# Down projections of the latents: one 512-column matmul for both parts of the input, halves added by VectorE

## The chip, the core and the metric

The kernel runs on one core of one Trainium2 chip. The metric is the device time of one execution in microseconds (us). A profiled execution gives the rows that are read below: TensorE matmuls (PE), TensorE weight loads (PEld), VectorE (DVE), ScalarE (ACT), GpSimd (POOL) and SyncE's DMA queue (SP). Each engine works through a queue of its own in a fixed order.

## What is computed

A two-layer backbone over 256 latent tokens and 256 context tokens of width 1024. Layer 0 mixes tokens by attention, layer 1 by a Fourier transform; each layer has a SwiGLU feed-forward before and one behind the mixing, so there are four feed-forwards. The first one treats latents and context, the other three the latents alone. The part that the change touches, cut from the reference:

```python
def swiglu(h, w_gu, w_d):
    g, u = jnp.split(h @ w_gu, 2, axis=-1)
    return (jax.nn.silu(g) * u) @ w_d

x = x + 0.5 * mx[2] * swiglu(modulate(rms_norm(x, norm_g[i, 0]), mx[0], mx[1]),
                             ffn1_w_gu[i], ffn1_w_d[i])
```

`w_gu` is 1024 x 5632 and `w_d` 2816 x 1024, in 32-bit floats. 2816 is 22 tiles of 128, called inner tiles here.

## The kernel before

**Products in parts.** TensorE works on rounded 32-bit operands. So that little is lost, each operand is split into a rounded part (`hi`, ScalarE's cast in `split`, L101) and the rest (`lo`, VectorE's subtraction, L102). A product is three matmuls into one bank of PSUM (`mm3`, L140 to L143): hi weights with the hi input, hi weights with the lo input, lo weights with the hi input. Each matmul loads its 128x128 block of weights anew, though the first two load the same block.

**A feed-forward** (`ffn`) runs in two halves of 11 inner tiles. In each half `gate_up` makes the 11 tiles of `silu(g) * u` (16 x 3 matmuls a tile, 258 columns: 256 tokens and two that carry the shift) and splits each into `h_hi` and `h_lo`. Then come eight down projections (`down`), one for each tile `dt` of the 1024 outputs: 11 x 3 matmuls of 256 columns into one bank (`dn`), and one VectorE instruction that multiplies the bank by the gate and adds it to the stream `xy` (L331). Such a run of eight down projections is called a down stretch here. The three feed-forwards of the latents alone have six of them.

**Behind the second half** of a feed-forward the next part waits for the stream: `after(dt)` scales the tile just finished into the next operand (`scaled`: `xop_hi` by ScalarE, L291, and `xop_lo` by VectorE, L292) and adds its square for the next norm (`sumsq`, ScalarE and GpSimd). Two places matter below. At the **first turn** the second feed-forward of layer 0 ends and the first of layer 1 begins: its `gate_up` needs all eight `xop` tiles. At the **second turn** that feed-forward ends and the Fourier mixing begins: it needs the norm's factors (`nv_l1m`, L251, made from the squares of all eight tiles).

**Beside it** VectorE splits the weights that come next (`wlo_d`, `wlo_gu`, `wlo_wf`: four instructions for each load), and works off the adaLN vectors of layer 1 (`products`, L193, named `junk` after its unused output: one instruction of 1024 columns for each 512 KB of the loaded `raw_m`). Raw weights, hi parts and lo parts live in rotating buffers: a DMA is issued when the buffer that it writes has been read.

**Order.** The program is written in the order above; the order in each engine's queue is set when the program is built, by a scheduler that follows estimated times and priorities (`URGENT` for the last additions to the stream, `AHEAD` for weights). On the chip each queue is strictly in order: an instruction that waits holds up all behind it.

Of the kernel before, what the change touches and what calls it, by code (L numbers as in the profile page):

```python
# [8 lines left out]
F32 = mybir.dt.float32  # L9
F32R = mybir.dt.float32r  # L10
# [4 lines left out]
P = 128  # L15
# [11 lines left out]
# first feed-forward: slices of its hidden tiles  # L27
SLICES = ((0, 6), (6, 12), (12, 17), (17, 22))
# order of the start: tiles of the first adaLN weights, xN pairs of input tiles, n norm, fN operands of a tile of d,
# gN first weights, c conditions  # L30
# [3 lines left out]
# adaLN work beside the feed-forwards: vectors of layer 1 done in the first one, VectorE time (us) per step, first tiles  # L34
# [6 lines left out]
# attention: slots of a head group's steps, offsets of the groups, order of the projections  # L41
# [5 lines left out]
# priorities of weight loads and of what the next phase waits for  # L47
AHEAD = 60
URGENT = 200
# pieces of a weight unit's split; buffers, lasting and added by phases  # L50
# [7 lines left out]
# columns of the packed small parameters (one row per partition)  # L58
# [5 lines left out]
# columns of the packed row vectors (broadcast to all partitions)  # L64
R_QG, R_KG, R_LQ1, R_LK1, R_LQ2, R_LK2 = range(0, 6 * HD, HD)
# columns of the shape-only tables
# [9 lines left out]
def tile_kernel(ctx: ExitStack, tc, xyT, small, rows, tables, w_mod0, w_mod, w_gu, w_d0, w_d, w_qkv, w_o, w_f, out):  # L76
# [22 lines left out]
    # ---------------------------------------------------------------- helpers  # L99
# [4 lines left out]
    # weights pass through rotating buffers; a phase that has the room adds some to the lasting ones  # L104
# [46 lines left out]
    # ---------------------------------------------------------------- constants, small inputs  # L151
# [13 lines left out]
    # ---------------------------------------------------------------- adaLN parameters  # L165
    mod = const.tile([P, 2, 2, 9, KT], F32, name="mod")  # layer, stream, which, d tile
    amul = const.tile([P, 2, 2, 3, KT], F32, name="amul")

    def first_products(dt, spool):
        """shift and scale of the first norm, both streams, for one tile of d: in rows"""  # L170
# [26 lines left out]
    def condition(sb, s):  # L197
        """silu of a condition, the same on all partitions"""
        nc.sync.dma_start(sb, rows[:, 6 * HD + s * D:6 * HD + (s + 1) * D].partition_broadcast(P))
        S.activation(sb, sb, AF.Silu)  # L200

    def ada_steps(pool, todo, conds):
        """one step per quarter of a vector's (transposed) weights"""
# [22 lines left out]
    # ---------------------------------------------------------------- norm pieces  # L226
    tails = {}  # the last d tile's squares
# [12 lines left out]
    def rstd_cols(acc, sl, name):  # L240
        """1/rms of each token, tokens on the partitions"""
# [668 lines left out]
```

## Time and profile before

| what | value |
|---|---|
| time, median of 3 runs | 1247.15 us (1245.64 to 1248.89) |
| span of the profiled execution | 1244.7 us |
| TensorE matmul busy | 1227.4 us (99%) |
| VectorE busy | 906.8 us (73%) |
| ScalarE busy | 549.3 us (44%) |

The times hold no separate time for the profiled execution; its span, from the first to the last instruction, is 2.4 us below the median. TensorE is busy nearly all the time as far as the page can say: ends of matmuls are modelled and overlap, so the distance between the starts of two matmuls tells more than the time of one. VectorE's 73% is a mean over stretches that differ.

### The profile page before, as it was taken

To read this page: it belongs to the slowest core of one execution; us is meant where nothing else is said; L and a number is where in the kernel's file an instruction comes from. 1 tells how busy PE (TensorE), PEld (TensorE's weight loads), DVE (VectorE), ACT (ScalarE), POOL (GpSimd) and SP (SyncE) were. 2 spreads that over 40 slices of the span, in tenths; PEclk is the share of its full clock that TensorE was granted. 3 is DMA by queue.
4 is the path that set the end of the run, shared out by engine and by line. 5 is a ranking of instruction groups with operands and counts; after the bars stand their busy time and mean duration, and the time that the engine had idled before them with its cause. 6 is when DMAs were issued, how large, how long until landed. Compare 5 with 4: busy or idle time off the path is not lost. (4 is left out here: it accounts for less than half of the span.)

```text
span 1244.7 us, 21253 instructions
## 1 busy us (share of the span) xinstructions
PE 1227.4 (99%) x8540; PEld 1121.5 (90%) x8540; DVE 906.8 (73%) x1761; ACT 549.3 (44%) x1207; POOL 102.0 (8%) x89
## 2 busy tenths in 40 slices
PE   9999999999999999999999999999999999999998
PEld 4688888888888889998899999999999999999998
DVE  1996985658874777777778687888688767766664
ACT  2342232223223455445645445555455545544552
POOL 1100000000001352340200000110000011000000
PEclk9999999999999999999999999999999999999999
DMA  9564574558881122122465686676686555536532
GB/s 364 217 239 166 204 248 136 198 184 308 314 309 68 69 102 102 69 68 69 170 223 198 234 302 226 211 301 227 211 310 240 171 195 183 180 127 244 189 117 81
DMA packets 37811, 241.94 MB, mean 194 GB/s; under 512 B 4224, under 2 KB 5376, under 8 KB 14672
## 3 DMA queue, kind: packets, MB, share of 16 engines
q1 hardware_dynamic: 37584, 240.25, 53.8%
q8 instruction: 67, 1.10, 0.3%
q0 software_dynamic: 128, 0.33, 0.2%
q14 instruction: 32, 0.26, 0.1%
HBM read 239.51 MB, written 1.05 MB: 193 GB/s over the span
## 5 line engine op out<-in xcount | busy, mean ns | idle before, releaser
L142 PE MATMUL gu<-xop_lo,whi_gu 128*128 128x258 f32 (+1 forms) x1408 | 440.2, 313 | 2.1 <-DVE xop_lo L292 2.1
L141 PE MATMUL gu<-xop_hi,whi_gu 128*128 128x258 f32 (+1 forms) x1408 | 439.0, 312 | 1.7 <-ACT whi_gu L101 1.4
L143 PE MATMUL gu<-xop_hi,wlo_gu 128*128 128x258 f32 (+1 forms) x1408 | 439.6, 312 | 0.4 <-DVE wlo_gu L102 0.2
L142 PEld LDWEIGHTS gu<-xop_lo,whi_gu 128*128 128x128 f32 x1408 | 268.0, 190 | 20.1 <-DVE xop_lo L292 2.6
L141 PEld LDWEIGHTS gu<-xop_hi,whi_gu 128*128 128x128 f32 x1408 | 268.0, 190 | 18.3 <-ACT whi_gu L101 1.7
L143 PEld LDWEIGHTS gu<-xop_hi,wlo_gu 128*128 128x128 f32 x1408 | 268.0, 190 | 17.2 <-DVE wlo_gu L102 1.3
L101 ACT CAST whi_gu<-raw_gu 128x512 fp32r<-128x512 f32 x352 | 194.7, 618 | 188.5 <-PE gu L142 102.4
L102 DVE TENSOR_TENSOR wlo_gu<-raw_gu,whi_gu 128x512 fp32r<-128x512 f32 x352 | 226.5, 689 | 60.1 <-ACT whi_gu L101 59.2
L142 PE MATMUL dn<-h_lo,whi_d 128*128 128x256 f32 (+1 forms) x724 | 219.6, 305 | 0.0
L143 PE MATMUL dn<-h_hi,wlo_d 128*128 128x256 f32 (+1 forms) x724 | 219.5, 305 | 0.0
L141 PE MATMUL dn<-h_hi,whi_d 128*128 128x256 f32 (+1 forms) x724 | 217.8, 305 | 0.2 <-DVE xy L331 0.2
L193 DVE SCALAR_TENSOR_TENSOR junk<-raw_m,cond_x 128x1024 f32<-128x1024 f32 x128 | 156.6, 1223 | 34.1 <-DMA raw_m<-in_w_mod 33.1
L101 ACT CAST whi_d<-raw_d 128x352 fp32r<-128x352 f32 (+2 forms) x256 | 105.9, 484 | 167.7 <-PE gu L142 84.5
L102 DVE TENSOR_TENSOR wlo_d<-raw_d,whi_d 128x352 fp32r<-128x352 f32 (+2 forms) x256 | 120.9, 524 | 58.6 <-ACT whi_d L101 58.6
L141 PEld LDWEIGHTS dn<-h_hi,whi_d 128*128 128x128 f32 x724 | 136.4, 189 | 6.8 <-PE dn L143 0.6
L142 PEld LDWEIGHTS dn<-h_lo,whi_d 128*128 128x128 f32 x724 | 136.9, 189 | 6.1
L143 PEld LDWEIGHTS dn<-h_hi,wlo_d 128*128 128x128 f32 x724 | 136.8, 189 | 6.1
L499 PE MATMUL pj<-whi_qkv,xop_hi 128*128 128x256 f32 x320 | 92.1, 288 | 0.6 <-DVE kr L545 0.5
L501 PE MATMUL pj<-whi_qkv,xop_lo 128*128 128x256 f32 x320 | 91.2, 286 | 1.4 <-DVE xop_lo L281 1.2
L331 DVE SCALAR_TENSOR_TENSOR xy<-dn,mod,xy 128x256 f32<-128x256 f32 x112 | 50.3, 477 | 57.5 <-PE dn L143 57.4
L500 PE MATMUL pj<-wlo_qkv,xop_hi 128*128 128x256 f32 x320 | 91.2, 285 | 0.9 <-DVE wlo_qkv L102 0.8
L101 ACT CAST h_hi<-hh 128x256 fp32r<-128x256 f32 (+1 forms) x88 | 40.3, 460 | 92.9 <-DVE hh L316 60.2
(220 smaller groups left out, 1412.5 us busy)
## 6 DMA issues: line engine op xcount, KB each, us to landing
raw_gu<-in_w_gu SPq DMA_DIRECT2D x88, 1024.0 KB, 5.2
raw_m<-in_w_mod SPq DMA_DIRECT2D x72, 1024.0 KB, 5.5
raw_d<-in_w_d SPq DMA_DIRECT2D x48, 704.0 KB, 4.1
raw_qkv<-in_w_qkv SPq DMA_DIRECT2D x12, 1024.0 KB, 4.8
raw_d<-in_w_d SPq DMA_DIRECT2D x8, 768.0 KB, 4.3
raw_d<-in_w_d SPq DMA_DIRECT2D x8, 640.0 KB, 5.3
raw_wo<-in_w_o SPq DMA_DIRECT2D x4, 1024.0 KB, 4.9
raw_wf<-in_w_f SPq DMA_DIRECT2D x4, 1024.0 KB, 6.9
```

The costliest lines, as they stand in the source:

```text
L101: S.copy(hi, src)
L102: V.tensor_sub(lo, src, hi.bitcast(F32))
L141: PE.matmul(ps, sh, mh, start=start, stop=False)
L142: PE.matmul(ps, sh, ml, start=False, stop=False)
L143: PE.matmul(ps, sl, mh, start=False, stop=stop)
L193: V.scalar_tensor_tensor(junk, w, 1.0, c, op0=ALU.mult, op1=ALU.mult, accum_out=out_col)
L331: V.scalar_tensor_tensor(xy[:, dt, so], ps[:, so.start - sl.start:so.stop - sl.start], mod[:, layer, s, 6 * f + 2, dt:dt + 1], xy[:, dt, s ...
L499: PE.matmul(ps[:, i], xh, wh, start=k == 0, stop=False)
L500: PE.matmul(ps[:, i], xh, wl, start=False, stop=False)
L501: PE.matmul(ps[:, i], xl, wh, start=False, stop=k == KT - 1)
```

## The change

In the three feed-forwards of the latents alone, `h_hi` and `h_lo` become the two halves of one tile `hp`, side by side for each inner tile. The rounded weights of an inner tile are then loaded once and both halves stream past them in one matmul of 512 columns, which fills a whole bank: its left half collects hi weights with the hi input, its right half hi weights with the lo input. The lo weights stream the hi input into the left half, as before. So a triple of 256-column matmuls becomes a pair, 512 and 256 columns. The sum of the two halves is left to VectorE: two instructions in the place of one, each adding one half to the stream, the right one first. The second of them needs the stream as the first has left it. The first feed-forward, with 512 tokens, keeps `down`.

```diff
+    def down_pairs(layer, f, dt, hi, lo, hp, urgent):
+        ps = (pB, pC)[dt % 2](f"dn_{layer}_{f}_{dt}")
+        for jj in range(JH):
+            c = slice(jj * P, (jj + 1) * P)
+            PE.matmul(ps, hi[:, c], hp[:, jj].rearrange("p s n -> p (s n)"), start=jj == 0, stop=False)
+            PE.matmul(ps[:, :NT], lo[:, c], hp[:, jj, 0], start=False, stop=jj == JH - 1)
+        with tc.high_priority(offset=URGENT) if urgent else nullcontext():
+            for i in (1, 0):
+                V.scalar_tensor_tensor(xy[:, dt, SX], ps[:, i * NT:(i + 1) * NT], mod[:, layer, 0, 6 * f + 2, dt:dt + 1],
+                                       xy[:, dt, SX], op0=ALU.mult, op1=ALU.add)
+
     def ffn(layer, f, rstd, fpool, after, step):
         for half in range(2):
-            h_hi = fpool.tile([P, JH, NT], F32R, tag="h_hi", name=f"h_hi_{layer}_{f}_{half}")
-            h_lo = fpool.tile([P, JH, NT], F32R, tag="h_lo", name=f"h_lo_{layer}_{f}_{half}")
+            hp = fpool.tile([P, JH, 2, NT], F32R, tag="hp", name=f"hp_{layer}_{f}_{half}")
+            h_hi, h_lo = hp[:, :, 0], hp[:, :, 1]
...
-                down(layer, f, dt, SX, hi, lo, 0, h_hi, h_lo, JH, None, half == 1)
+                down_pairs(layer, f, dt, hi, lo, hp, half == 1)
```

The rest of the diff takes comments away. The order of the DMA queue and of GpSimd's queue is that of before, instruction for instruction; on TensorE, VectorE and ScalarE it moves from the second feed-forward of layer 0 on. Names below: `dn_0_1_0` is the bank of layer 0, second feed-forward, output tile 0; `whi_d0110` the hi part of the weights of layer 0, second feed-forward, second half, tile 0; `gu_1_0_0` a gate-up bank of layer 1.

TensorE, second half of layer 0's second feed-forward, where the bank of output tile 0 gets its last two or three matmuls. Before:

```order
L141 MATMUL dn_0_1_2_0_7751<-h_hi_0_1_1_6819,whi_d0112_7741 128x256
L142 MATMUL dn_0_1_0_0_7641<-h_lo_0_1_1_6820,whi_d0110_7631 128x256
L143 MATMUL dn_0_1_0_0_7641<-h_hi_0_1_1_6819,wlo_d0110_7632 128x256
L142 MATMUL dn_0_1_1_0_7693<-h_lo_0_1_1_6820,whi_d0111_7683 128x256
L143 MATMUL dn_0_1_1_0_7693<-h_hi_0_1_1_6819,wlo_d0111_7684 128x256
```

TensorE, the same place after the change:

```order
L340 MATMUL dn_0_1_2_7649<-hp_0_1_1_6738,whi_d0112_7639 128x512
L340 MATMUL dn_0_1_0_7559<-hp_0_1_1_6738,whi_d0110_7549 128x512
L341 MATMUL dn_0_1_0_7559<-hp_0_1_1_6738,wlo_d0110_7550 128x256
L340 MATMUL dn_0_1_1_7601<-hp_0_1_1_6738,whi_d0111_7591 128x512
L341 MATMUL dn_0_1_1_7601<-hp_0_1_1_6738,wlo_d0111_7592 128x256
```

The bank's last matmul was the 77th of the stretch; it is now the 59th, behind 28 pairs and two matmuls of 512 columns, its own among them.

VectorE, the first turn: the last additions to the stream, up to the last `xop_lo` (the row ahead of `nv_l1f0`, which begins the next norm). Before:

```order
L102 TENSOR_TENSOR wlo_gu101_8154<-raw_gu101_8151,whi_gu101_8153 128x512 x4
L292 SCALAR_TENSOR_TENSOR xop_lo_104<-xy_86,amul_99,xop_hi_103 128x256
L331 SCALAR_TENSOR_TENSOR xy_86<-dn_0_1_7_0_8017,mod_98,xy_86 128x256
L193 SCALAR_TENSOR_TENSOR junk_8296,mcols_1_6_8293<-raw_m160_8294,cond_x_102 128x1024
L102 TENSOR_TENSOR wlo_gu102_8225<-raw_gu102_8222,whi_gu102_8224 128x512 x4
L292 SCALAR_TENSOR_TENSOR xop_lo_104<-xy_86,amul_99,xop_hi_103 128x256
```

VectorE, the same place after the change:

```order
L344 SCALAR_TENSOR_TENSOR xy_86<-dn_0_1_7_7865,mod_98,xy_86 128x256
L102 TENSOR_TENSOR wlo_gu102_8062<-raw_gu102_8059,whi_gu102_8061 128x512
L344 SCALAR_TENSOR_TENSOR xy_86<-dn_0_1_6_7823,mod_98,xy_86 128x256
L102 TENSOR_TENSOR wlo_gu102_8062<-raw_gu102_8059,whi_gu102_8061 128x512 x3
L193 SCALAR_TENSOR_TENSOR junk_8133,mcols_1_6_8130<-raw_m160_8131,cond_x_102 128x1024
L292 SCALAR_TENSOR_TENSOR xop_lo_104<-xy_86,amul_99,xop_hi_103 128x256
L344 SCALAR_TENSOR_TENSOR xy_86<-dn_0_1_7_7865,mod_98,xy_86 128x256
L292 SCALAR_TENSOR_TENSOR xop_lo_104<-xy_86,amul_99,xop_hi_103 128x256
L193 SCALAR_TENSOR_TENSOR junk_8135,mcols_1_6_8130<-raw_m160_8131,cond_x_102 128x1024
L292 SCALAR_TENSOR_TENSOR xop_lo_104<-xy_86,amul_99,xop_hi_103 128x256
```

Each addition stands twice, and the second of the two adaLN instructions of `raw_m160`, which stood behind the last `xop_lo`, now stands ahead of it. From the first addition of the stretch to the last `xop_lo` there are three of them before, four after; all else in that piece of the queue is the same work.

VectorE, the rows behind that. Before:

```order
L251 TENSOR_SCALAR nv_l1f0_8068<-ss_l1f0_8063 128x2
L102 TENSOR_TENSOR wlo_gu103_8303<-raw_gu103_8300,whi_gu103_8302 128x512 x4
L314 TENSOR_TENSOR gus_8145<-gu_1_0_0_8092,rstd_l1f0_8075 128x512
L193 SCALAR_TENSOR_TENSOR junk_8515,mcols_1_6_8293<-raw_m161_8513,cond_x_102 128x1024
L102 TENSOR_TENSOR wlo_gu104_8374<-raw_gu104_8371,whi_gu104_8373 128x512 x2
```

VectorE, the same place after the change:

```order
L251 TENSOR_SCALAR nv_l1f0_7906<-ss_l1f0_7901 128x2
L193 SCALAR_TENSOR_TENSOR junk_8352,mcols_1_6_8130<-raw_m161_8350,cond_x_102 128x1024
L193 SCALAR_TENSOR_TENSOR junk_8354,mcols_1_6_8130<-raw_m161_8350,cond_x_102 128x1024
L102 TENSOR_TENSOR wlo_gu103_8140<-raw_gu103_8137,whi_gu103_8139 128x512 x2
L314 TENSOR_TENSOR gus_7982<-gu_1_0_0_7929,rstd_l1f0_7913 128x512
```

`gus`, which empties the gate-up bank of the first tile, stood ahead of the instructions on `raw_m161`; both of them now stand ahead of it. There are two gate-up banks, so the third tile waits for it.

## Rows read from the trace of the kernel before

**Rows 1.** The page: busy time by engine, share of the span, instructions.

```profile
PE 1227.4 (99%) x8540; PEld 1121.5 (90%) x8540; DVE 906.8 (73%) x1761; ACT 549.3 (44%) x1207; POOL 102.0 (8%) x89
```

**Rows 2.** Timeline of PE, ends of a 256-column down stretch: start, us, instruction.

```profile
781.97 0.28 PE L141 MATMUL dn<-h_hi,whi_d 128*128 128x256 f32 x1
...
813.07 0.28 PE L143 MATMUL dn<-h_hi,wlo_d 128*128 128x256 f32 x1
```

**Rows 3.** Timeline of PE, first feed-forward: ends of 512-column down and gate-up stretches.

```profile
113.46 0.40 PE L141 MATMUL dn<-h_hi,whi_d 128*128 128x512 f32 x1
...
145.89 0.39 PE L143 MATMUL dn<-h_hi,wlo_d 128*128 128x512 f32 x1
146.12 0.40 PE L141 MATMUL gu<-xop_hi,whi_gu 128*128 128x512 f32 x1
...
213.09 0.39 PE L143 MATMUL gu<-xop_hi,wlo_gu 128*128 128x512 f32 x1
```

**Rows 4.** The page's group of the additions: busy, mean ns, idle before, releaser.

```profile
L331 DVE SCALAR_TENSOR_TENSOR xy<-dn,mod,xy 128x256 f32<-128x256 f32 x112 | 50.3, 477 | 57.5 <-PE dn L143 57.4
```

**Rows 5.** Windows: us, then busy PE, PEld, DVE, ACT, POOL, clock, DMA.

```profile
687.06:718.21 31.15, 31.15 (x265) 31.15 (x264) 22.90 (x48) 15.03 (x35) 0.00 (x0) 1.00 0.65 231
791.31:821.41 30.10, 29.40 (x247) 29.11 (x246) 30.10 (x56) 20.48 (x48) 6.40 (x6) 1.00 0.77 273
982.23:1010.51 28.28, 28.17 (x239) 27.99 (x237) 27.53 (x54) 20.22 (x46) 6.81 (x6) 1.00 0.67 243
```

**Rows 6.** Timeline of DVE, first turn; in brackets idle time before, and its releaser.

```profile
791.31 0.88 DVE L331 SCALAR_TENSOR_TENSOR xy<-dn,mod,xy 128x256 f32<-128x256 f32 x2 [3.21 <-PE dn L143]
...
812.25 0.47 DVE L331 SCALAR_TENSOR_TENSOR xy<-dn,mod,xy 128x256 f32<-128x256 f32 x1
812.64 2.48 DVE L102 TENSOR_TENSOR wlo_gu<-raw_gu,whi_gu 128x512 fp32r<-128x512 f32 x4
815.05 0.96 DVE L292 SCALAR_TENSOR_TENSOR xop_lo<-xy,amul,xop_hi 128x256 fp32r<-128x256 f32 x1
815.93 0.47 DVE L331 SCALAR_TENSOR_TENSOR xy<-dn,mod,xy 128x256 f32<-128x256 f32 x1
816.33 1.21 DVE L193 SCALAR_TENSOR_TENSOR junk<-raw_m,cond_x 128x1024 f32<-128x1024 f32 x1
...
819.88 0.47 DVE L292 SCALAR_TENSOR_TENSOR xop_lo<-xy,amul,xop_hi 128x256 fp32r<-128x256 f32 x1
...
826.76 0.68 DVE L314 TENSOR_TENSOR gus<-gu,rstd_l1f 128x512 f32<-128x512 f32 x1
828.97 1.22 DVE L193 SCALAR_TENSOR_TENSOR junk<-raw_m,cond_x 128x1024 f32<-128x1024 f32 x1 [1.52 <-DMA raw_m<-in_w_mod]
```

**Rows 7.** Timelines of PE and PEld, first turn: the two instructions that waited.

```profile
820.40 0.39 PE L142 MATMUL gu<-xop_lo,whi_gu 128*128 128x258 f32 x1 [0.67 <-DVE xop_lo L292]
...
827.50 0.19 PEld L141 LDWEIGHTS gu<-xop_hi,whi_gu 128*128 128x128 f32 x1 [0.35 <-DVE gus L314]
```

**Rows 8.** Timeline of the DMA queue, first turn: the load of `raw_m161`.

```profile
821.52 0.33 SPq L208 DMA_DIRECT2D raw_m<-in_w_mod  x1
```

**Rows 9.** The page's DMA groups: KB each, median us from issue to landing.

```profile
raw_m<-in_w_mod SPq DMA_DIRECT2D x72, 1024.0 KB, 5.5
```

**Rows 10.** Timeline of DVE, second turn.

```profile
982.23 0.88 DVE L331 SCALAR_TENSOR_TENSOR xy<-dn,mod,xy 128x256 f32<-128x256 f32 x2 [3.26 <-PE dn L143]
...
1010.51 0.16 DVE L251 TENSOR_SCALAR nv_l1m<-ss_l1m 128x2 f32<-128x2 f32 x1
```

**Rows 11.** Windows of the turn into layer 0's second feed-forward: columns as in rows 5.

```profile
614.00:618.00 4.00, 1.65 (x12) 1.25 (x11) 4.00 (x9) 4.00 (x10) 1.79 (x2) 0.99 0.71 264
618.00:622.00 4.00, 3.88 (x18) 3.26 (x17) 4.00 (x6) 3.02 (x9) 3.07 (x4) 0.59 0.76 262
```

**Rows 12.** Timeline of PE: the last matmul of the program.

```profile
1240.91 0.28 PE L143 MATMUL dn<-h_hi,wlo_d 128*128 128x256 f32 x1
```

**Rows 13.** The last addition, from DVE's timeline.

```profile
1241.23 0.48 DVE L331 SCALAR_TENSOR_TENSOR xy<-dn,mod,xy 128x256 f32<-128x256 f32 x1 [3.39 <-PE dn L143]
```

## Prediction

> **What bounds the kernel now.** I read the busy times first [rows 1]: TensorE is busy for 1227.4 of 1244.7 us, in 8540 matmuls. So the change can gain only by making a triple of matmuls shorter than it is, and can lose wherever TensorE has to stand. The pitch, from the start of one matmul to the start of the next, comes from the ends of whole stretches. A down stretch of 256 columns runs from 781.97 to 813.07 [rows 2], and its 8 x 11 x 3 = 264 matmuls have 263 pitches: 31.10 / 263 = 118.3 ns. With 512 columns it is (145.89 - 113.46) / 143 = 226.8 ns in a down stretch and (213.09 - 146.12) / 287 = 233.3 ns in a gate-up stretch [rows 3]. Twice 118.3 is 236.6 ns: doubling the columns nearly doubles the time.
>
> Then VectorE. All additions together had 57.5 us of idle time ahead of them, nearly all of it waiting for TensorE's bank [rows 4]. In a first half VectorE is busy for 22.90 of 31.15 us, and TensorE all the time [first window of rows 5]. At the turns it is otherwise. From the first addition to the next norm's factors VectorE is busy for 30.10 of 30.10 us at the first turn and for 27.53 of 28.28 at the second [other windows of rows 5]: there VectorE is what ends last. TensorE stands 0.67 us for the last `xop_lo`, and its third gate-up tile waits 0.35 us for `gus` [rows 7]. So a microsecond more on VectorE in these two stretches is a microsecond more of the program.
>
> **The matmuls.** 528 triples (six stretches of 8 x 11) become pairs. A triple takes 3 x 118.3 = 354.8 ns. A pair takes 118.3 plus 226.8 to 233.3, that is 345.1 to 351.6 ns, the mid 348.4. It saves 6.4 ns, between 3.2 and 9.7. If the matmul of 256 columns also fell to half of 226.8, behind a load that has more time, the pair would take 340.2 and save 14.6. One stretch (88 pairs) gains 0.56 us (0.28 to 1.28). In the two stretches ahead of the turns this gain is lost to the wait behind them. Four stretches keep it: the first halves of the two feed-forwards before the turns and both of the last one. **-2.3 us** (-1.1 to -5.1). The 528 weight loads that fall away give nothing of their own, since loads run beside matmuls and are inside the pitch.
>
> The pages have a rule for this. The Trainium skill, "TensorE: Matmul & The Clock Gate", section on the back-to-back issue gap, gives the gap as the columns at 2.4 GHz plus about 2.5 ns, so 109.2 ns for 256 and 215.8 for 512. By it only one overhead of 2.5 ns is saved per triple, 0.22 us a stretch, and the four stretches would give -0.9. The trace has 9 to 18 ns more than the page at either size [rows 2, 3], so I go by the rows.
>
> **The additions in the four stretches without a turn behind them** cost nothing but at the very end. They are 32 more instructions; one takes 0.39 us from start to start (812.64 - 812.25) [rows 6], so eight take 3.1 us, and VectorE has 31.15 - 22.90 = 8.25 us idle in such a stretch. If that cover were gone, it would be 3.1 us each. The end of the program is the exception: the second addition needs the stream as the first leaves it, and the last one stands in the open, 0.32 us behind the start of the last matmul [rows 12, 13]. One more of 0.48 us: **+0.5** (0.4 to 0.6).
>
> **The first turn.** Three things make VectorE's queue later. First, its first addition waits for the last matmul of the stretch's first bank. That one was the 77th, which starts 76 x 118.3 ns = 8.99 us behind 781.97; the addition began at 791.31, 9.34 behind, so 0.35 us later than that matmul's start [rows 2, 6]. Now it is the 59th, behind 28 pairs and two matmuls of 512: 28 x 0.3484 + 2 x 0.230 = 10.21 us. That is +1.2, and VectorE is full from there on, so nothing takes it up. Second, eight more additions: +3.1. Third, one more adaLN instruction stands ahead of the last `xop_lo`, of 1.21 us [rows 6]: +1.2. Together +5.5: the last `xop_lo` would begin at 825.4 instead of 819.88, and the matmul that waited 0.67 us would wait some 6.
>
> What is late next? The load of `raw_m161` is issued when the second instruction on `raw_m160` has read the buffer, at 821.52 [rows 8]. This instruction now ends about where the last `xop_lo` begins, at 825.4. The median load lands 5.5 us behind its issue [rows 9], so at 830.9; before it took up to 828.97, 7.45 us, as far as VectorE's wait for it tells [rows 6]. Two instructions on it (2 x 1.2) and two pieces of `wlo_gu` (a quarter of 2.41 each, 1.2 in all) now stand ahead of `gus`, which comes at 834.5 instead of 826.76 [rows 6]. Third gate-up tile: 834.5 - 826.8 = **+7.7**, with the 5.5 of above inside it. The lower end is 4.5: the pieces fall so that `gus` doesn't wait and the lateness of the last `xop_lo` is 1 less, since rows of the same form differ by as much (`xop_lo` took 0.96 at 815.05, 0.47 at 819.88 [rows 6]). The upper end is 9.6: the load takes 7.45 again.
>
> **The second turn.** Here the bank's last matmul was the 63rd and is the 50th (24 pairs and a matmul of 512 ahead of it): 24 x 0.3484 + 0.230 - 62 x 0.1183 = +1.26. The additions cost +3.1, and 0.7 of the 0.75 us of idle time (28.28 - 27.53) [rows 5] may be filled. `nv_l1m`, at 1010.51 [rows 10], comes 1.26 + 3.1 - 0.7 = 3.6 us later behind the stretch's start: **+3.6** (2.6, an error of 1 as above, to 4.4, nothing filled).
>
> **The clock.** At an earlier turn TensorE was busy for 1.65 of 4.00 us at a granted clock of 0.99; in the 4 us behind, busy again, it was granted 0.59, so mostly 1.2 instead of 2.4 GHz [rows 11]. A stand of 4 to 6 us may bring that here. At the first turn it costs nothing while `gus` sets the pace. At the second I take half of what 4 us at 0.59 lose, 0.41 x 4 / 2 = **+0.8** (0 to 1.7).
>
> **The sum:** -2.3 + 0.5 + 7.7 + 3.6 + 0.8 = +10.3. The span goes from 1244.7 to 1255.0. The median was 2.45 above that span, so the time is **1257.4 us**, 0.8% slower.
>
> **Rivals.** (1) *The additions hide and the pairs gain*: faster, in contrast to the forecast. VectorE's many waits for TensorE [rows 4] speak for it. If such waits were inside the turns as well, only the matmuls would count: six stretches at their best, 6 x 1.28, less 0.5 for the end give -7.2, 1240.0 (with the mid pitch -2.9, 1244.3). It decides from about 4 us of idle time in a turn's window, enough for the eight additions and the later start; the windows have 0.00 and 0.75 [rows 5], so it has little. Chance 0.06. (2) *The turns cost only their lower ends*, with the matmuls at their best: -5.1 + 4.5 + 2.6 + 0.5 + 0 = +2.5, 1249.7. VectorE's uneven durations speak for it; that three separate terms must fall the same way speaks against. 0.12. (3) *Nothing is gained by the loads saved*: the pair takes 351.6 ns, as gate-up's pitch of 233.3 has it [rows 3], so the change hardly does what it might at all: -1.1 for -2.3, all else as forecast, 1258.6. It is bound by columns then, which are the same 768. 0.14. The Trainium skill's gap formula, same page and section as above, comes to nearly this, 1258.8; the rows at 512 columns lie between. (4) *The load lands as late as it did, and the clock falls in full*: -2.3 + 9.6 + 4.4 + 1.7 + 0.5 = +13.9, 1261.1. For it speaks the one load at this place; the 72 loads' median against. 0.10.
>
> **How the numbers follow.** The forecast has 0.58. From 1250 to 1262 lie the forecast, rivals 3 and 4 and a part of rival 2; left out are rival 1, most of rival 2 and some for a turn that is worse than its bounds, some 0.18 together. 0.3% is 3.7 us, about what a measurement of this kernel can tell from no change. Faster by more than that (under 1243.4) is rival 1 with the better of its two pitches, 0.04 of its 0.06; within is the rest of it and rival 2, 0.14; slower is what is left, 0.82.
>
> **What would show it.** Right: a pair's pitch of 345 to 352 ns and down stretches of some 30.6 us without a stand; no idle time on VectorE between the first addition and the norm's factors at both turns; one stand of about 6 us on TensorE at the first turn, ended by the last `xop_lo`, then one ended by `gus`; `nv_l1m` 3.6 us later counted from the start of its down stretch; first halves without a stand. Wrong: a pair under 340 ns, or VectorE idle in the turns (then rival 1); a raw load that lands 7 us or more behind its issue, with VectorE idle ahead of `raw_m161` (rival 4); a last `xop_lo` less than 4 us late (rival 2). What I can't see is whether an addition takes longer with a bank that TensorE is filling on its other side; the rows of before have none of that kind.

## The result

The changed kernel takes 1259.8 us (median of 4 runs, 1257.4 to 1263.1) against 1247.9 for the kernel before in the same sitting: a ratio of 1.0094, 95% interval 1.0079 to 1.0110. Timed once more (experiment 11), the ratio was 1.0089, 1.0071 to 1.0106. The change makes the kernel slower by some 11 to 12 us. Forecast were 1257.4 us, +10.3.

The spans of single traces differ also for a reason that is not the change. The first down stretch of the latents begins at 687.06 us in the trace of before and at 691.48 in that of after, but over all traces of this case, the program ahead of it being the same, it begins anywhere from 686.4 to 692.2, at 692.2 in the fastest kernel of all. (Only in experiments 5 and 8 do VectorE and ScalarE have another order, in the last 16 us or so ahead of it.) So traces are compared from that start on. The starts of the six down stretches cut the rest into six pieces. The first matmuls of the stretches and the last matmul of the program, from TensorE's timeline of after (start, us, instruction; the row at 921.38 ends the third stretch):

```profile
691.48 0.39 PE L340 MATMUL dn<-hp,whi_d 128*128 128x512 f32 x1
...
786.77 0.40 PE L340 MATMUL dn<-hp,whi_d 128*128 128x512 f32 x1
...
890.78 0.40 PE L340 MATMUL dn<-hp,whi_d 128*128 128x512 f32 x1
...
921.38 0.28 PE L341 MATMUL dn<-hp,wlo_d 128*128 128x256 f32 x1
...
985.18 0.39 PE L340 MATMUL dn<-hp,whi_d 128*128 128x512 f32 x1
...
1130.38 0.39 PE L340 MATMUL dn<-hp,whi_d 128*128 128x512 f32 x1
...
1224.67 0.40 PE L340 MATMUL dn<-hp,whi_d 128*128 128x512 f32 x1
...
1255.17 0.28 PE L341 MATMUL dn<-hp,wlo_d 128*128 128x256 f32 x1
```

The same starts before are 687.06, 781.97 [rows 2], 879.69, 974.56, 1114.89 and 1209.80, with the end at 1244.71. The pieces in us, with the difference from before for each kernel of this study:

| kernel | 1: first half, l0 | 2: first turn | 3: first half, l1 | 4: second turn | 5: last feed-forward | 6: last stretch, end | sum | ratio of times, 95% |
|---|---|---|---|---|---|---|---|---|
| before, length | 94.9 | 97.7 | 94.9 | 140.3 | 94.9 | 34.9 | 557.7 | |
| the change | +0.4 | +6.3 | -0.5 | +4.9 | -0.6 | -0.1 | +10.4 | 1.0094 (1.0079 to 1.0110) |
| e11, the change again | -0.6 | +7.3 | -0.4 | +4.8 | -0.6 | -0.1 | +10.4 | 1.0089 (1.0071 to 1.0106) |
| e1, four stretches | -0.6 | 0.0 | -0.5 | +0.3 | -0.6 | -0.1 | -1.5 | 0.9992 (0.9979 to 1.0005) |
| e2, two turns | 0.0 | +6.6 | 0.0 | +4.0 | 0.0 | 0.0 | +10.5 | 1.0098 (1.0083 to 1.0113) |
| e3, one addition | -0.6 | +2.4 | -0.5 | +4.9 | -0.6 | -0.6 | +5.0 | 1.0027 (1.0016 to 1.0038) |
| e4, additions alone | -0.1 | +6.3 | 0.0 | +4.6 | -0.1 | +0.4 | +11.1 | 1.0118 (1.0098 to 1.0138) |
| e5, adaLN away | +2.4 | +4.1 | -0.3 | +1.2 | -0.6 | -0.1 | +6.7 | 1.0066 (1.0045 to 1.0087) |
| e6, step later | -0.6 | +6.5 | -0.5 | +4.2 | -0.6 | -0.1 | +8.9 | 1.0072 (1.0055 to 1.0089) |
| e7, clock kept | -0.6 | +10.0 | -0.4 | +4.2 | -0.6 | -0.1 | +12.6 | 1.0085 (1.0066 to 1.0104) |
| e8, four and away | +1.9 | -0.9 | +1.0 | +0.1 | -0.6 | -0.1 | +1.4 | 1.0006 (0.9995 to 1.0017) |
| e9, clock both | +2.1 | +5.3 | -0.5 | +2.3 | -0.7 | -0.1 | +8.4 | 1.0045 (1.0027 to 1.0063) |
| e10, four, no tail | -0.6 | -0.9 | -0.6 | +0.1 | -0.6 | -0.6 | -3.1 | 0.9975 (0.9964 to 0.9985) |
| e12, step alone | 0.0 | -0.8 | 0.0 | -0.1 | 0.0 | 0.0 | -0.9 | 1.0004 (0.9994 to 1.0013) |

In e8 one matmul of the third stretch stands 6 us ahead of the others; its pieces are counted from the second, at 881.22. Pieces that two kernels have alike agree to 0.1 us in most rows. The exceptions are told below: stands (an engine waits and does nothing) behind late loads in piece 1 of the change and of e9 and in piece 2 of e7, and in piece 2 of the change 6.3 in one trace and 7.3 in the other, with half the clock for longer in the second.

### The profile page after: what moved, and what is told of

Read it like the earlier page. It is cut to its first block, busy times and chain, and to the rows that moved or that the text cites. A ratio compares the mean times of both kernels' runs of the same rounds, so it can differ in the third digit from the quotient of the medians.

```text
span 1259.5 us, 20259 instructions
## 1 busy us (share of the span) xinstructions
PE 1233.1 (98%) x8012; PEld 1102.4 (88%) x8012; DVE 923.1 (73%) x1809; ACT 548.7 (44%) x1207; POOL 105.2 (8%) x89
## 4 chain that ended last, share of the span: by engine, by line
PE 87%; DVE 8%; DMA 3%; issue 1%; ACT 1%; POOL 1%; SPq 0%; DVEq 0%; ACTq 0%; POOLq 0%
PE gu L143 16%; PE gu L142 16%; PE gu L141 16%; PE dn L340 7%; PE dn L341 4%; PE dn L141 3%; PE dn L142 3%; PE dn L143 3%; PE pj L511 3%; PE pj L512 2%; PE pj L513 2%; DMA raw_m<-in_w_mod 2%; PE psr L175 2%; DVE wlo_gu L102 1%; DVE wlo_d L102 1%; PE s L607 1%
## 5 line engine op out<-in xcount | busy, mean ns | idle before, releaser
L340 PE MATMUL dn<-hp,whi_d 128*128 128x512 f32 x528 | 183.5, 393 | 0.0
L341 PE MATMUL dn<-hp,wlo_d 128*128 128x256 f32 x528 | 145.9, 280 | 0.0
L340 PEld LDWEIGHTS dn<-hp,whi_d 128*128 128x128 f32 x528 | 98.3, 188 | 21.2
L341 PEld LDWEIGHTS dn<-hp,wlo_d 128*128 128x128 f32 x528 | 99.4, 188 | 1.6 <-DVE wlo_d L102 0.3
L142 PE MATMUL dn<-h_lo,whi_d 128*128 128x512 f32 (+1 forms) x196 | 71.8, 368 | 0.0
L143 PE MATMUL dn<-h_hi,wlo_d 128*128 128x512 f32 (+1 forms) x196 | 71.7, 368 | 0.0
L141 PE MATMUL dn<-h_hi,whi_d 128*128 128x512 f32 (+1 forms) x196 | 70.8, 368 | 0.1
L344 DVE SCALAR_TENSOR_TENSOR xy<-dn,mod,xy 128x256 f32<-128x256 f32 x96 | 44.3, 476 | 30.9 <-PE dn L341 30.6
```

The source lines that it names most:

```text
L141: PE.matmul(ps, sh, mh, start=start, stop=False)
L142: PE.matmul(ps, sh, ml, start=False, stop=False)
L143: PE.matmul(ps, sl, mh, start=False, stop=stop)
L340: PE.matmul(ps, hi[:, c], hp[:, jj].rearrange("p s n -> p (s n)"), start=jj == 0, stop=False)
L341: PE.matmul(ps[:, :NT], lo[:, c], hp[:, jj, 0], start=False, stop=jj == JH - 1)
L344: V.scalar_tensor_tensor(xy[:, dt, SX], ps[:, i * NT:(i + 1) * NT], mod[:, layer, 0, 6 * f + 2, dt:dt + 1], xy[:, dt, SX], op0=ALU.mult, o ...
```

## The profile after

The busy times and the group of the additions, from the page of after, to be held against [rows 1] and [rows 4]:

```profile
PE 1233.1 (98%) x8012; PEld 1102.4 (88%) x8012; DVE 923.1 (73%) x1809; ACT 548.7 (44%) x1207; POOL 105.2 (8%) x89
...
L344 DVE SCALAR_TENSOR_TENSOR xy<-dn,mod,xy 128x256 f32<-128x256 f32 x96 | 44.3, 476 | 30.9 <-PE dn L341 30.6
```

528 matmuls are gone and TensorE's busy time has still risen: busy counts a matmul at half clock twice as long. An addition takes 476 ns as before. That its bank is now twice as wide, 512 columns for 256, costs it nothing. The idle time ahead of the additions is ended by L341, the bank's last matmul, so these rows don't settle what the prediction had left open, a bank that TensorE is filling on its other side.

**A pair.** The third stretch runs from 890.78 to 921.38, 30.60 us in which 175 pitches lie: 87 pairs and one matmul of 512 columns. (30.60 - 0.23) / 87 = 349.1 ns a pair, against 354.8 for a triple. In the last stretch, from 1224.67 to 1255.17, it is (30.50 - 0.23) / 87 = 347.9.

**The first turn.** VectorE's timeline of after, from the first addition to `gus`:

```profile
797.27 0.88 DVE L344 SCALAR_TENSOR_TENSOR xy<-dn,mod,xy 128x256 f32<-128x256 f32 x2 [4.37 <-PE dn L341]
...
829.32 0.48 DVE L292 SCALAR_TENSOR_TENSOR xop_lo<-xy,amul,xop_hi 128x256 fp32r<-128x256 f32 x1
831.37 0.16 DVE L251 TENSOR_SCALAR nv_l1f<-ss_l1f 128x2 f32<-128x2 f32 x1 [1.56 <-PE ss_l1f L248]
834.24 1.22 DVE L193 SCALAR_TENSOR_TENSOR junk<-raw_m,cond_x 128x1024 f32<-128x1024 f32 x1 [2.71 <-DMA raw_m<-in_w_mod]
...
837.86 0.68 DVE L314 TENSOR_TENSOR gus<-gu,rstd_l1f 128x512 f32<-128x512 f32 x1
```

Counted from the start of the stretch (786.77, before 781.97), the first addition stands at 10.50 instead of 9.34, the last `xop_lo` at 42.55 instead of 37.91, `gus` at 51.09 instead of 44.79 [rows 6]. The load that holds up the row at 834.24 was issued at 829.43, when the last instruction on `raw_m160` had ended (DMA queue of after):

```profile
829.43 0.33 SPq L208 DMA_DIRECT2D raw_m<-in_w_mod  x1
```

TensorE's three stands in this turn, from its timeline, and ScalarE's `xop_hi` of output tile 6, right ahead of the square of that tile:

```profile
825.43 0.58 PE L247 MATMUL ss_l1f<-ones,ssacc_after 128*128 128x1 f32 x2 [3.20 <-POOL ssacc_after L238]
...
827.53 0.58 PE L142 MATMUL gu<-xop_lo,whi_gu 128*128 128x258 f32 x1 [1.51 <-DVE xop_lo L292]
...
838.60 0.39 PE L141 MATMUL gu<-xop_hi,whi_gu 128*128 128x258 f32 x1 [0.47 <-DVE gus L314]
```

```profile
823.63 0.51 ACT L291 ACTIVATE xop_hi<-xy,amul 128x256 fp32r<-128x256 f32 x1 [1.84 <-DVE xy L344]
```

The longest is not ended by `xop_lo` but by GpSimd's sum of squares: a matmul for the norm's factors (`ss_l1f`, which sums the squares over the partitions) stands in TensorE's queue ahead of gate-up matmuls, and the square of output tile 6 waits for that tile's second addition.

**The second turn.** VectorE and TensorE, from their timelines of after:

```profile
994.11 0.88 DVE L344 SCALAR_TENSOR_TENSOR xy<-dn,mod,xy 128x256 f32<-128x256 f32 x2 [4.37 <-PE dn L341]
...
1024.93 0.16 DVE L251 TENSOR_SCALAR nv_l1m<-ss_l1m 128x2 f32<-128x2 f32 x1 [0.20 <-PE ss_l1m L248]
```

```profile
1020.18 0.59 PE L247 MATMUL ss_l1m<-ones,ssacc_after 128*128 128x1 f32 x2 [2.10 <-POOL ssacc_after L238]
...
1025.15 0.58 PE L141 MATMUL z<-fd_hi,xop_hi 128*128 128x258 f32 x1 [0.32 <-DVE nv_l1m L251]
```

`nv_l1m` stands 39.75 us behind the start of its down stretch, before 35.95 (1010.51 - 974.56) [rows 10]. Here too the stand is ended by the sum of squares. Windows of after (columns as in [rows 5]) show a first half, the clock behind both stands, and the first turn as a whole:

```profile
691.48:722.09 30.61, 30.61 (x177) 26.81 (x176) 24.17 (x52) 15.11 (x35) 0.00 (x0) 1.00 0.64 228
797.27:831.37 34.10, 29.30 (x170) 25.92 (x169) 32.53 (x66) 20.41 (x48) 8.14 (x6) 0.90 0.76 273
826.00:830.00 4.00, 2.49 (x12) 2.48 (x12) 3.80 (x8) 0.82 (x2) 0.00 (x0) 0.50 0.73 264
...
1020.00:1024.00 4.00, 3.78 (x17) 3.70 (x18) 4.00 (x9) 1.54 (x4) 0.12 (x1) 0.50 0.55 195
```

0.50 is 1.2 of 2.4 GHz. VectorE is busy for 32.53 of 34.10 us of the first turn; the missing 1.56 are its wait for TensorE's sum right ahead of `nv_l1f`. At the second turn it stands 0.69 us for ScalarE's `td_hi` and the 0.20 above.

**The first half of layer 0.** The change's first trace lost 0.4 us here, its second gained 0.6. Both are the same program; in the first, an adaLN instruction waited for a late load with `gus` behind it. VectorE, then TensorE, of after:

```profile
742.89 1.22 DVE L193 SCALAR_TENSOR_TENSOR junk<-raw_m,cond_x 128x1024 f32<-128x1024 f32 x1 [3.40 <-DMA raw_m<-in_w_mod]
```

```profile
745.99 0.39 PE L141 MATMUL gu<-xop_hi,whi_gu 128*128 128x258 f32 x1 [0.50 <-DVE gus L314]
```

## The experiments

The theory was that of the prediction: the pairs gain some 0.55 us a stretch wherever VectorE has time, and at the two turns the instructions that are added to a full VectorE make the end late. Against it stood that the banks' later ends or the clock are the price, that the four other stretches lose too, and that loads decide.

**1. Pairs in four stretches.** In `ffn`:

```diff
-                down_pairs(layer, f, dt, hi, lo, hp, half == 1)
+                if half == 0 or (layer, f) == (1, 1):
+                    down_pairs(layer, f, dt, hi, lo, hp, half == 1)
+                else:
+                    down(layer, f, dt, SX, hi, lo, 0, h_hi, h_lo, JH, None, half == 1)
```

> Pairs only in the four down stretches with no turn behind them (both of the last feed-forward, the first halves of the two ahead of it); the two stretches ahead of the turns keep triples and one addition. Theory (the loss is VectorE's, at the two turns; a stretch of pairs gains 0.55 us): 4 x -0.55 + 0.5 for the last addition = -1.7 us against the kernel before, no stand of TensorE over 1 us at either turn. Rival (the additions cost in these stretches too, through gus that comes late in the gate-up tiles beside them): 0 to +3 us.

Measured: ratio 0.9992 (0.9979 to 1.0005); in the trace -1.5 us, -0.6, -0.5 and -0.6 in the three pieces of whole stretches, -0.1 at the end, no new stand at the turns. The pairs gain what was forecast and the additions are hidden there. The runs alone would not tell it from no change.

**2. Pairs ahead of the two turns only.** The same edit with the condition `half == 1 and (layer, f) != (1, 1)`.

> Pairs only in the two stretches ahead of the turns. Theory: +6.3 at the first turn and +4.9 at the second, as the changed kernel's trace has them from the start of one down stretch to the start of the next, together +11.2 us against the kernel before. Rival (what the changed kernel loses comes partly from the other four stretches or from the program's start): +7 to +9 us.

Measured: 1.0098, and +10.5 in the trace, all of it in the pieces of the turns. The whole loss is there. The rival is out.

**3. One addition.** The stream gets the left half alone:

```diff
-            for i in (1, 0):
+            for i in (0,):
```

> All pairs as in the change, but the addition of the right half of the bank is left out (the product of hi weights with the lo input never reaches the stream). VectorE's queue is then that of the kernel before. Theory (instructions on VectorE are the price, the later last matmul of the first bank a small one): 4 x -0.55, +1.2 at the first turn, +0.6 at the second: -0.4 us against the kernel before. Rival (the price is that banks are finished later, and the clock behind it): +5 to +9 us.

Measured: 1.0027 (1.0016 to 1.0038), +5.0 in the trace. Neither the theory's -0.4 nor, as a whole, the rival's +5 to +9 by the later bank: the first turn costs 2.4 instead of 1.2, and the second turn the full 4.9, with not one addition more than before. But VectorE's queue is not that of the kernel before, as was expected: from the first addition to the last `xop_lo` it has the same instructions at either turn, in another order. So what is measured is the later bank together with that order. (The runs have +2.0 to +4.7 us for the trace's +5.0.) The chain there, in rows of ScalarE and VectorE and a window of this kernel:

```profile
1006.77 2.18 ACT L101 CAST whi_wf<-raw_wf 128x512 fp32r<-128x512 f32 x4 [1.95 <-DMA raw_wf<-in_w_f]
```

```profile
1013.62 0.47 DVE L292 SCALAR_TENSOR_TENSOR xop_lo<-xy,amul,xop_hi 128x256 fp32r<-128x256 f32 x1
1015.40 0.16 DVE L251 TENSOR_SCALAR nv_l1m<-ss_l1m 128x2 f32<-128x2 f32 x1 [1.31 <-PE ss_l1m L248]
```

```profile
1012.00:1016.00 4.00, 3.68 (x19) 3.59 (x18) 2.25 (x6) 0.46 (x2) 0.36 (x1) 0.50 0.87 279
```

The last `xop_lo` is 2.0 us late (37.36 behind the stretch's start, before 35.36). The second adaLN instruction of the stretch ends 2.6 us later behind the stretch's start than before (22.96 for 20.41), the first load of `raw_wf` is issued 2.1 later (23.06 for 20.95), ScalarE's cast waits 1.95 us for it, and `xop_hi` and the square of tile 6 stand behind that cast in ScalarE's queue. TensorE then stands 1.44 us for the sum of squares, its clock falls to 0.50, the Fourier matmuls queued ahead of the last sum take nearly twice their time, and VectorE waits 1.31 us for that sum: `nv_l1m` is 3.2 us late, and matmuls at half clock behind it lose 1.7 more.

**4. The additions alone.** Triples again, the lo input into the right half (the first inner tile of a bank keeps the 512 columns, which opens both halves):

```diff
-            PE.matmul(ps, hi[:, c], hp[:, jj].rearrange("p s n -> p (s n)"), start=jj == 0, stop=False)
+            if jj == 0:
+                PE.matmul(ps, hi[:, c], hp[:, jj].rearrange("p s n -> p (s n)"), start=True, stop=False)
+            else:
+                for i in range(2):
+                    PE.matmul(ps[:, i * NT:(i + 1) * NT], hi[:, c], hp[:, jj, i], start=False, stop=False)
```

> Two additions as in the change and its order on VectorE, but triples of 256 columns (only the first inner tile of a bank keeps the 512-column matmul). Theory: no gain by matmuls, and the first bank is finished as early as before: 3.1 + 1.2 at the first turn and 0.8 more behind it through gus, 2.4 at the second and 0.6 by the clock, 0.5 at the end, together +8.6 us against the kernel before. Rival (512-column matmuls themselves or the later bank make the loss): 0 to +3 us.

Measured: 1.0118 (1.0098 to 1.0138), +11.1 in the trace: +6.3 and +4.6 at the turns, +0.4 at the end. That is more than the sum that was expected, and as much at either turn as with the pairs. Experiments 3 and 4 together: at the second turn the later bank with its order on VectorE costs 4.9, the additions alone 4.6, both together 4.9. The prices do not add. At the first turn it is 2.4, 6.3 and 6.3 to 7.3, so there the additions (and the adaLN instructions that change places with them) carry nearly all.

**5. adaLN steps away from the turns.**

```diff
-                step(ROOM1)
+                step(0.0 if half else 2 * ROOM1)
```

> The change as it is (all pairs, two additions), but the adaLN steps that stood beside the second halves' down stretches are taken up in the first halves' instead (room 1.5 us a tile there, 0 in the second). Two instructions of 1.21 us fewer stand on VectorE at each turn. Theory (full VectorE is what ends late, by instructions and by the loads whose buffers it frees): about +3 us at the first turn instead of +6.3, +1.5 at the second instead of +4.9, in all +3 us against the kernel before. Rival (the later bank and the halved clock are the price whatever stands on VectorE): +9 us or more.

Measured: 1.0066, +6.7 in the trace. The turns come out near the theory, +4.1 for its 3 and +1.2 for its 1.5, with all pairs and additions in place. By the trace the rival is out; the runs alone, +5.6 to +10.9 us, leave it room. At the second turn the first addition stands at 9.28, later than the change's 8.93, and yet the turn costs 1.2: there VectorE's load is the price. At the first turn less is shown, since the order on TensorE has changed as well and the first addition stands at 8.56, where the change has 10.50 and the kernel before 9.34. And the steps are not free where they went: +2.4 in the first half of layer 0, against -0.6 for the change without the stand.

**6. No adaLN step on the first gate-up tile.**

```diff
-                if f == 0 or half * JH + jj >= ADA_FROM:
+                if half * JH + jj >= (1 if f == 0 else ADA_FROM):
```

> The change as it is, but the first gate-up tile of each half takes no adaLN step. One adaLN instruction then stands behind the last xop_lo at the first turn again, gus no longer stands behind the load of raw_m161, and no adaLN instruction is left at the second turn. Theory: +4 us at the first turn instead of +6.3 (the last xop_lo alone sets it, not gus), +2 at the second instead of +4.9, in all +4.5 us. Rival (gus is late for another reason than the load of raw_m161): the first turn stays at +6 us, in all +7.

Measured: 1.0072, +8.9 in the trace, worse than the theory and nearer to the rival. At the first turn the last `xop_lo` comes 1.2 us earlier than in the change (41.34 behind the start) and `gus` no longer waits for `raw_m161`, yet it comes at 50.94, the change's 51.09. TensorE's stand, two windows behind it, and ScalarE's copy of the norm's factors, which `gus` needs:

```profile
821.22 0.59 PE L247 MATMUL ss_l1f<-ones,ssacc_after 128*128 128x1 f32 x2 [3.13 <-POOL ssacc_after L238]
```

```profile
822.00:826.00 4.00, 3.84 (x18) 3.84 (x19) 3.65 (x9) 0.82 (x2) 0.27 (x1) 0.50 0.74 262
826.00:830.00 4.00, 4.00 (x20) 4.00 (x20) 0.00 (x0) 0.00 (x0) 0.44 (x1) 0.50 0.76 262
```

```profile
830.98 0.37 ACT L264 COPY rstd_l1f<-rb_l1f 128x256 f32<-128x256 f32 x1 [7.63 <-PE rb_l1f L261]
```

The matmul that spreads the factors (`rb_l1f`) stands in TensorE's queue behind gate-up matmuls, and these run at half clock for 8 us. With the load out of the way the clock is next: `gus` ends at 51.62, and TensorE begins its third gate-up tile 0.5 us behind that without a stand.

**7. Matmuls into the stand at the second turn.** In `rstd_cols`, ahead of the sums:

```diff
+        if name == "l1m":
+            for k, n in ((5, 10), (6, 8)):
+                for _ in range(n):
+                    PE.matmul(ps[:, NT:], xop_hi[:, k, :P], xop_hi[:, k, :NT], start=True, stop=True)
```

> The change as it is, with 18 idle-filling matmuls of 256 columns on TensorE at the second turn, ahead of the matmul that waits for GpSimd's sum of squares (10 that need xop tile 5, 8 that need tile 6; their result is not read). Theory: VectorE's lateness (3.7 us) stays, the halved clock behind the stand goes: second turn +3.8 us instead of +4.9, in all -1 us against the changed kernel. Rival A (the clock is no price at all): second turn +4.9 or more. Rival B (the clock is the whole price): second turn +2 or less.

Measured: the second turn +4.2 instead of the change's +4.9 and +4.8. The theory had +3.8; rival B is out. Rival A is not: the last `xop_lo` stands 0.65 us earlier here than in the change (38.44 for 39.08), and experiment 2, with VectorE as early as here and no such matmuls, has +4.0. So this run doesn't tell what the clock costs; experiment 9 does. The clock held only at first (0.63 in the window from 1026 to 1030). The whole kernel, 1.0085, can't be told from the change: in this trace the first turn, whose order is the change's, took +10.0, since ScalarE's cast of a gate-up weight waited 2.54 us for its load there, where the change's waited 0.30, with `xop_hi` of the next tile behind it. Loads move the turn by that much from one run to another.

**8. Four stretches, and adaLN steps moved.** The condition of experiment 1 with the edits of 5 and 6.

> Pairs in the four stretches only, as in the first experiment, and the adaLN steps out of the second halves' down stretches and off the first gate-up tile of each half. Theory: -1.7 by the pairs, -1 at the first turn where TensorE stood 0.67 and 0.35 us before, -1 to -2.4 at the second, where the norm's factors come up to two instructions of 1.21 us earlier: -3.7 to -5 us against the kernel before. Rival (the turns of the kernel before are set by chains that VectorE's load does not move): -1.7 us.

Measured: 1.0006 (0.9995 to 1.0017), +1.4 in the trace. Theory and rival are both out, since neither has the first halves: the first turn gains its 0.9, the second nothing (the rival's half), and the first halves lose 1.9 and 1.0. A first half of this kernel as a window, and TensorE's wait right behind it:

```profile
688.00:719.00 31.00, 30.80 (x176) 26.47 (x174) 28.00 (x62) 13.17 (x32) 0.00 (x0) 1.00 0.79 280
```

```profile
720.08 0.39 PE L141 MATMUL gu<-xop_hi,whi_gu 128*128 128x258 f32 x1 [1.28 <-ACT whi_gu L101]
```

VectorE is at 28.00 of 31.00 there, where the change has 24.17 of 30.61: the cover is used up, and what ends late is the next weights.

**9. Both clocks.** The kernel of experiment 6 with the edit of 7 for both turns (12 and 10 matmuls).

> The kernel of e6_step_later with idle-filling matmuls at both turns (12 that need xop tile 5 and 10 that need tile 6, result not read), ahead of the matmul that waits for the sum of squares. In e6 the trace has TensorE at a granted clock of 0.50 for some 9 us behind its stand of 3.3 us at the first turn, with 40 matmuls of gate-up at 215 instead of 120 ns, 3.8 us, and gus behind them. Theory (behind VectorE's lateness the halved clock is the next price): first turn +3 us instead of +6.5, second +2 instead of +4.2, in all +3 us against the kernel before. Rival (the clock only fills time in which something else is awaited): first turn +6, second +4, in all +8.

Measured: 1.0045, +8.4 in the trace, which as a whole is the rival's sum (the runs have +3.4 to +7.9), though +2.1 of it are in the first half of layer 0, with stands of 1.8 us for `gus`, as in the first trace of the change. At the second turn +2.3 instead of 4.2, as the theory has it: the last `xop_lo` stands at 36.94 here and at 36.98 in experiment 6, so VectorE is equally late, and a window over the same place has a granted clock of 1.00 here and 0.52 there. These are the rows, of this kernel and then of experiment 6:

```profile
1019.00:1023.00 4.00, 3.68 (x28) 3.40 (x28) 2.31 (x7) 0.91 (x3) 0.71 (x1) 1.00 0.67 240
```

```profile
1018.00:1022.00 4.00, 3.68 (x20) 3.59 (x18) 1.22 (x5) 1.35 (x5) 0.71 (x1) 0.52 0.82 307
```

2.0 us at the second turn (142.6 for 144.6, one trace each) are the clock's. At the first turn it is +5.3 instead of 6.5, not the +3 that was expected: the fall of the clock came later and shorter (0.76 and 0.81 in windows from 826 to 834), and the 22 matmuls take 2.7 us of TensorE themselves.

**10. Four stretches, no tail.** Experiment 1 with the edit of 6, and the last output tile of the program as before:

```diff
+                if half == 0 or ((layer, f) == (1, 1) and dt < KT - 1):
```

> Pairs in the four stretches as in the first experiment, but triples and one addition for the last output tile of the program, and no adaLN step on the first gate-up tile of the two feed-forwards that have one there. Theory: -1.5 as the first experiment's trace has it, -0.4 by the last addition, up to -0.9 at the first turn (two adaLN instructions ahead of the last xop_lo instead of three), nothing in the first halves: -2 to -2.8 us against the kernel before. Rival (steps that are moved cost elsewhere, as in e8): 0 to +1 us.

Measured: 1244.95 us, ratio 0.9975 (0.9964 to 0.9985), and -3.1 in the trace: -0.6 in each of the three whole pieces, -0.9 at the first turn, -0.6 at the end. This is faster than both kernels, by 3 us against the one before and some 14 against the change.

**11. The change again.**

> The changed kernel once more, for a second trace: which parts of the two turns come again. Theory: from the start of the first down stretch of the latents' feed-forwards to the end +10.4 us against the kernel before, of these +6.3 at the first turn and +4.5 (4.0 to 4.9) at the second; the 4.4 us that the first trace had ahead of that stretch do not come again. Rival (they belong to the change): the trace has 3 to 4 us more ahead of that stretch again.

Measured: 1.0089, +10.4 in the trace, +7.3 and +4.8 at the turns. The sum is as expected, the first turn costs 1.0 more. Up to some 44 us behind the start of its stretch TensorE is at one with the first trace; from there the half clock lasts longer. The second trace, then the first, about 44 us behind the start:

```profile
828.00:832.00 4.00, 4.00 (x21) 4.00 (x21) 0.22 (x2) 0.00 (x0) 0.71 (x1) 0.50 0.76 262
```

```profile
830.00:834.00 4.00, 4.00 (x32) 4.00 (x31) 0.16 (x1) 0.00 (x0) 0.71 (x1) 0.88 0.75 264
```

The third gate-up tile begins at 52.96 instead of 51.83, 0.5 us behind the end of `gus` and without a stand: here TensorE's own half clock sets the pace, and not `gus`. The first stretch began at 690.12. That start lies between those of the other kernels, so nothing of it is laid to the change.

**12. The step alone.** The kernel before with only the edit of 6.

> The kernel before (triples everywhere), with only the adaLN step taken off the first gate-up tile of the two feed-forwards that have one there, as in e10. Theory (e10's gain is the four stretches and the last addition, -2.2, and this step at the first turn, -0.85, as its trace has them): 96.9 instead of 97.7 us at the first turn, all other stretches as before, -0.8 us in all. Rival (the step is what e10 gains by): -3 us.

Measured: -0.8 at the first turn and nothing elsewhere in the trace; the runs show no gain, 1.0004 (0.9994 to 1.0013). So the step is not what experiment 10 gains by: -2.2 of its -3.1 are the pairs and the last addition.

## Why the prediction was right, step by step

- **The sum.** Forecast +10.3, in the trace +10.4. That they agree to 0.1 is luck: the first turn came 1.4 us under its forecast, the second 0.5 over it, and the other pieces gained 0.8 instead of 1.8 (1.7 in the second trace, without the late load, and there the first turn was only 0.4 under).
- **The pitch.** Forecast 348.4 ns a pair, measured 347.9 to 349.1. Forecast 0.56 us a stretch, measured 0.4 to 0.6. Rival 3 (351.6) is out. The Trainium skill, "TensorE: Matmul & The Clock Gate", section on the back-to-back issue gap, has its formula for an isolated matmul; worked out from it, 325.0 ns for the pair and a saving of 2.5 are an estimate. The rows, of a stream with a weight load for each matmul, have 349.1 and a saving of 5.7, so the measurement decides against that estimate.
- **Additions hidden in the four stretches, +0.5 at the end.** Right: experiment 1 has no loss there, and the last piece gains 0.6 with one addition (experiment 3) and 0.1 with two.
- **The first turn, forecast +7.7, measured +6.3 and +7.3.** The first addition was forecast 10.56 behind the stretch's start and stands at 10.50. The last `xop_lo` was forecast 5.5 late and is 4.6 late; 0.8 of the sum of 4.3 for nine more instructions was taken up by rows that were shorter than before. The load took 4.8 us to the first instruction on it, forecast 5.5. `gus` behind it decides in the first trace, as forecast; in the second (experiment 11) it is TensorE at half clock. What was not foreseen is whom TensorE waits for: I had one stand of about 6 us ended by `xop_lo`, and it is 3.20 for the sum of squares and 1.51 for `xop_lo`. I had read only the wait that was there before [rows 7], not what else stands in TensorE's queue at that place. "No idle time on VectorE" did not hold either: it stands 1.56 us at the first turn and 0.89 at the second. Rival 1 does not follow from that: the first wait is for a sum that is late itself, and a wait of 0.62 us for the same `td_hi` was there before.
- **The second turn, forecast 3.6 and 0.8 for the clock, measured 3.8 and 1.1** (4.0 and 0.8 the second time). The sum is right, its working is not. I had added the later bank (+1.26), the additions (+3.1) and taken off 0.7 of idle time, which says that without the additions 0.6 would remain. Experiment 3 has 4.9, with no addition more though in another order on VectorE. And the 0.7 of idle time that I took off was not filled (0.69 us of it stayed, for `td_hi`); in the trace the rows other than the additions took 0.7 less in all, so that the sum came out by luck. Missing in my chain were the way through the buffers (a later read, a later load, a cast in ScalarE's queue ahead of `xop_hi` and the square) and the stand for the sum of squares with the clock behind it.
- **The clock at the first turn, forecast 0 while `gus` sets the pace.** Right for the first trace only. In the second the half clock lasted some 4 us longer and TensorE was late by itself: +7.3 instead of +6.3. Experiment 6 shows the same, since with `gus` freed from the load the half clock takes its place and the turn costs the same.
- **The start of the span.** Some 1 to 1.5 us of the 11 to 12 of the runs are not in the pieces (+10.4). Starts scatter by 5 us from trace to trace; what the rest is stays open.

How the loss at the second turn grows with VectorE's lateness is seen best across the kernels (last `xop_lo` and `nv_l1m` in us behind the stretch's start, the whole piece):

| kernel | last `xop_lo` | `nv_l1m` | piece 4 |
|---|---|---|---|
| before | 35.36 | 35.95 | 140.3 |
| e5 | 35.84 | 36.90 | 141.5 |
| e9 (clock held) | 36.94 | 38.21 | 142.6 |
| e6 | 36.98 | 38.92 | 144.6 |
| e3 | 37.36 | 39.14 | 145.2 |
| e4 | 38.23 | 40.34 | 144.9 |
| e2 | 38.40 | 38.97 | 144.3 |
| e7 | 38.44 | 38.84 | 144.5 |
| the change | 39.08 | 39.75 | 145.2 |
| e11 | 39.38 | 39.95 | 145.1 |

It is a step, not a slope: from 1.6 us of lateness on, wherever the clock was let fall, it costs 4 to 5 us, and up to 2.4 us more lateness cost nothing on top. That is read from one trace each, and the kernels differ in more than this lateness.

## What to carry to other kernels

A saving on the full engine is worth only what the stretch behind it lets through: put such a change where the other engine has idle time, and leave it out where that engine ends last; here four stretches of six, less the very last tile and with one adaLN step taken elsewhere, turn a loss of 0.9% into a gain of 0.25%. Work moved out of a full stretch is not free in the next one: hold its time against the idle time there after all other changes. And when two causes make the same wait late, test each alone before adding their prices: behind a stand that also drops the clock, either one can cost the whole.

## What was not expected of the hardware

A stand of TensorE of 1.44 us at the second turn of experiment 3 and one of 3.13 us at the first turn of experiment 6 came with a fall of the granted clock to 0.50 (1.2 GHz), which held for 9 to 10 us of busy work; the kernel before, which stands 0.67 us at the first turn [rows 7], kept a clock of 1.00 behind it. How long it lasts differs between two traces of one kernel, as experiment 11 shows. And with matmuls of no use in the stand the clock held at the second turn and fell later and less at the first. The rows show the before and after of the falls, not the rule by which they come.
